# The feed-forward part of a hybrid decoder layer in two phases: gate and up for all feature pairs, then the down projection as seven block products

## Chip, cores and metric

One core of a Trainium2 chip runs the program. The metric is device microseconds per execution, lower is better; before and after are timed in several runs each, and the median counts.

## What is computed

One layer: a time-mixing part, a pooling part and an output projection give `h` (1024 tokens x 1024 features), and then this feed-forward part, on which the change works:

```python
D_FF = -(-8 * D_MODEL // (3 * 256)) * 256          # 2816 = 22 x 128
f = (jax.nn.silu(h @ ffn_gate[i]) * (h @ ffn_up[i])) @ ffn_down[i]
e = jax.nn.sigmoid(h @ pl_gate[i]) * (p[i] @ pl_proj[i])
h = layer_norm(ALPHA * h + f + e, ln2_g[i], ln2_b[i])
```

## The kernel before, in words

**Splits.** Every operand of a matmul is held as two `float32r` parts, high and low: `split` (line 789) casts the fp32 value on ScalarE (line 790) and subtracts the cast from it on VectorE (line 791). A product of two operands is then three matmuls (line 49): high x high, high x low, low x high. `wsplit` (799) splits into a tile of the pool `w`; `load` (794) brings 128x512 fp32 values into one of six `raw` buffers over SP's DMA queue. The numbers of buffers stand in `NB` (775): 6 `raw`, 4 `g`, 4 `pu`, 8 `w`, 4 `a`.

**Gate and up.** The 22 feature tiles of 128 go in 11 pairs. For each pair `gate_up` (961) calls `seven` (925) twice, for gate and for up. `seven` multiplies a 2x2 block matrix of weights (two feature tiles, two halves of the 1024 inputs) with a 2x2 block matrix of activations (input halves, token halves) by seven products where the plain way has eight: sums and differences of the weights are made on VectorE, those of the activations were made once (`tb1` to `tb4`), and each product is 12 matmuls of 128x512 into one PSUM bank. Gate uses the three banks of pool `mm`, up those of pool `dn` (five). VectorE adds the products into the four blocks of the result; gate goes through Silu on ScalarE, and up times gate is split at once (line 976) into the tiles `ahl`.

**Down.** `down` (995) takes a pair's two feature tiles: for each half `cf` of the 1024 outputs it loads and splits two weight tiles (`down_w`, 982), and for each of eight token tiles makes 6 matmuls into a bank (`down_tile`, 985), which VectorE adds into `acc` (line 993), the fp32 sum of 1024 tokens x 1024 outputs in SBUF. The down of a pair stands in `mid` (1029) of the next one, between its gate and its up; the last two pairs are done together at the end, 12 matmuls to a bank, with the final norm `fin` (1003) behind each token tile. `late` (1011) puts scale, bias and the embedding term onto `acc`, 16 VectorE instructions in each of three pairs.

**Order.** The engines run in program order each; the framework's scheduler sets that order when the program is built, and its semaphores make an instruction wait for what it reads and for buffers that come free. TensorE's list follows the code; the lists of VectorE, ScalarE and SP are interleaved.

Of the kernel before, what the change touches and what calls it, by code (L numbers as in the profile page):

```python
# [9 lines left out]
F32 = mybir.dt.float32  # L10
F32R = mybir.dt.float32r
AF = mybir.ActivationFunctionType
ALU = mybir.AluOpType
# [7 lines left out]
KT = 8  # L21
# [3 lines left out]
NFF = 22  # L25
# [17 lines left out]
def hybrid_layer(ctx, tc, x, pT, w_in, cols, rows, lora, gl, pool_w, w_out,  # L43
                 ff_gate, ff_up, ff_down, pl_proj, pl_gate, out, dbg=_no):
    nc = tc.nc
    V, S, G, PE = nc.vector, nc.scalar, nc.gpsimd, nc.tensor

    def mm(o, l, r, a, z):
        PE.matmul(o, lhsT=l, rhs=r, start=a, stop=z)  # L49
# [5 lines left out]
    dp = ctx.enter_context(tc.tile_pool(name="scr", bufs=2, space=DRAM))  # L55

    hp = ctx.enter_context(tc.tile_pool(name="act", bufs=4))
# [18 lines left out]
    for h in range(2):  # L76
        r = slice(64 * h, 64 * h + 64)
# [41 lines left out]
    e_d = dp.tile([T, D], F32, name="e_d", bufs=1)  # L119
    pe_d = dp.tile([T, D], F32, name="pe_d", bufs=1)  # L120
    m_d = dp.tile([T, D], F32, name="m_d", bufs=1)
    rkv_d = dp.tile([3 * NP, 128, 512], F32, name="rkv_d", bufs=1)
    st8 = cq.tile([128, NP, 64], F32, name="st8")
    mmp = ctx.enter_context(tc.tile_pool(name="mm", bufs=3, space=PSUM))

    def act_tiles(nm):
        return [hp.tile([128, KT, 512], F32R, name=f"{nm}{i}", tag="act") for i in range(4)]
# [631 lines left out]
    dnp = ctx.enter_context(tc.tile_pool(name="dnb", bufs=5, space=PSUM, reuse_waits="tile"))  # L759

    acc = [sp.tile([128, D], F32, name=f"acc{tt}", tag="acc", bufs=8) for tt in range(8)]
# [7 lines left out]
    for tt in range(4, 8):  # L769
        mix(tt)  # L770
    ostk.close()
    bp = ctx.enter_context(tc.tile_pool(name="bp", bufs=1, side="right", reuse_waits="tile"))


    NB = {"raw": 6, "g": 4, "pu": 4, "w": 8, "a": 4}
# [1 line left out]
    def small(tag, nm, dt=F32):  # L777
        return sp.tile([128, 512], dt, name=nm, tag=tag, bufs=NB[tag])

    def wide(tag, nm, dt=F32R):  # L780
        return sp.tile([128, 2, 512], dt, name=nm, tag=tag, bufs=NB[tag])

    def flat(t):
        return t.rearrange("p x c -> p (x c)")
# [4 lines left out]
    def split(h, l, r):  # L789
        S.copy(h, r)  # L790
        V.tensor_tensor(l, r, h.bitcast(F32), ALU.subtract)  # L791
        return h, l

    def load(src, nm):
        r = small("raw", nm)
        nc.sync.dma_start(r.rearrange("p (k c) -> p k c", c=src.shape[2]) if len(src.shape) == 3 else r, src)
        return r

    def wsplit(r, nm):
        t = wide("w", nm)  # L800
        return split(t[:, 0, :], t[:, 1, :], r)


    b12, b11, b21, b22 = act_tiles("h1")
# [7 lines left out]
    def brow(i, nm, tag):  # L812
        t = flat(wide(tag, nm, F32))
        nc.sync.dma_start(t, rows[i:i + 1, :].to_broadcast([128, D]))
        return t
# [21 lines left out]
    for i, k in enumerate((2, 3)):  # L837
        hl = [t23[:, 4 * i + 2 * x:4 * i + 2 * x + 2, :].rearrange("p c f -> p (c f)") for x in range(2)]
        for cf in range(2):
            r = load(w_out[128 * k:128 * k + 128, 512 * cf:512 * cf + 512], "w23r")  # L840
# [3 lines left out]
    for i in range(2):  # L844
        r = load(ya_d[2 + i, :, 512:1024], "y23")
        split(yh[:, 512 * i:512 * i + 512], yl[:, 512 * i:512 * i + 512], r)
    for tt in range(4, 8):
        for cf in range(2):
            cs = slice(512 * cf, 512 * cf + 512)
            ps = mmp.tile([128, 512], F32, name="pm", tag="mm")  # L850
            for i, (wh, wl) in enumerate(w23):
                tsl = slice(512 * i + 128 * tt - 512, 512 * i + 128 * tt - 384)
# [105 lines left out]
        evict(0, 1, prod(w3, b22, "p3"), u4, u4)  # L958
        evict(1, 0, prod(w4, tb4, "p4"), u3, u3)

    def gate_up(f, ahl, mid):
        g = {}

        def keep_gate(i, t, ps, u, c):
            d = g[i, t] = small("g", "gs")
            V.tensor_tensor(d, ps, u, ALU.add)  # L966
            S.activation(d, d, AF.Silu)

        def keep_up(i, t, ps, u, c):
            d = g[i, t]  # L970
            c = small("pu", "c") if c is None else c
            V.tensor_tensor(c, ps, u, ALU.add)
            V.tensor_tensor(d, c, d, ALU.mult)
            ah, al = ahl[i]
            sl = slice(512 * t, 512 * t + 512)
            split(ah[:, sl], al[:, sl], d)

        seven(ff_gate, f, lambda nm: mmp.tile([128, 512], F32, name=nm, tag="mm"), keep_gate)
        mid()
        seven(ff_up, f, lambda nm: dnp.tile([128, 512], F32, name=nm, tag="dn"), keep_up)  # L980

    def down_w(fs, cf):
        return [wsplit(load(ff_down[128 * f:128 * f + 128, 512 * cf:512 * cf + 512], "wdr"), "wd") for f in fs]

    def down_tile(ahl, ws, tt, cf):
        tsl = slice(128 * tt, 128 * tt + 128)
        cs = slice(512 * cf, 512 * cf + 512)
        ps = dnp.tile([128, 512], F32, name="pd", tag="dn")
        for n, ((ah, al), (wh, wl)) in enumerate(zip(ahl, ws)):
            mm(ps, ah[:, tsl], wh, n == 0, False)  # L990
            mm(ps, ah[:, tsl], wl, False, False)
            mm(ps, al[:, tsl], wh, False, n == len(ahl) - 1)
        V.tensor_tensor(acc[tt][:, cs], ps, acc[tt][:, cs], ALU.add)  # L993

    def down(fs, ahl):
        for cf in range(2):
            ws = down_w(fs, cf)
            for tt in range(8):
                down_tile(ahl, ws, tt, cf)

    grows = []

    def fin(tt):
        a = acc[tt]
        (m,), (rs,) = stats(sp, [a])
        V.scalar_tensor_tensor(a, a, m, grows[0], ALU.subtract, ALU.mult)
        V.scalar_tensor_tensor(a, a, rs, grows[1], ALU.mult, ALU.add)
        nc.sync.dma_start(out[128 * tt:128 * tt + 128, :], a)


    def late(f):
        if f not in (2, 4, 6):
            return
        for cf in range(2):
            cs = slice(512 * cf, 512 * cf + 512)
            r = None
            if f < 6:
                r = load(rows[1 + f // 2:2 + f // 2, cs].to_broadcast([128, 512]), "rw")
                S.activation(r, r, AF.Copy, scale=ALPHA)
            for tt in range(8):  # L1020
                a = acc[tt][:, cs]
                t = load(e_d[128 * tt:128 * tt + 128, cs], "er") if r is None else r
                V.tensor_tensor(a, a, t, ALU.mult if f == 2 else ALU.add)

    prev = []
    for f in range(0, NFF - 2, 2):
        ahl = [[None, None], [None, None]]

        def mid():
            late(f)  # L1030
            if prev:
                down(*prev.pop())
            for i in range(2):
                for x in range(2):
                    ahl[i][x] = flat(wide("a", "ahl"[0:2] + "hl"[x]))

        gate_up(f, ahl, mid)
        prev.append(((f, f + 1), ahl))


    f = NFF - 2
    ahl = [[None, None], [None, None]]

    def mid():
        t = hp.tile([128, KT, 512], F32R, name="alast", tag="act")
        for i in range(2):
            for x in range(2):
                ahl[i][x] = t[:, 4 * i + 2 * x:4 * i + 2 * x + 2, :].rearrange("p c f -> p (c f)")

    gate_up(f, ahl, mid)  # L1050
    (fs, ahl0), = prev
    ws = [down_w(fs, cf) for cf in range(2)]
    t = hp.tile([128, KT, 512], F32R, name="wlast", tag="act")
    for cf in range(2):
        for i in range(2):
            r = load(ff_down[128 * (f + i):128 * (f + i) + 128, 512 * cf:512 * cf + 512], "wdr")
            ws[cf].append(split(t[:, 4 * cf + 2 * i, :], t[:, 4 * cf + 2 * i + 1, :], r))
    grows += [brow(4, "g2", "w"), brow(5, "b2", "w")]
    for tt in range(8):
        for cf in range(2):  # L1060
            down_tile(ahl0 + ahl, ws[cf], tt, cf)
        fin(tt)


_SHAPES = [
# [46 lines left out]
```

## Time and profile before

| | us |
|---|---|
| median of 3 runs | 1390.58 (1387.95 to 1393.26) |
| the profiled execution | 1389.85 |
| its span in the trace | 1388.1 |
| TensorE matmul busy (PE) | 1333.3, 96% of the span |
| VectorE busy (DVE) | 1012.0, 73% |
| ScalarE busy (ACT) | 487.8, 35% |
| moved by DMA | 122.89 MB, 89 GB/s over the span |

PE is the matmul row of TensorE and PEld its weight loads, DVE is VectorE, ACT is ScalarE, SP the engine whose queue issues the DMAs. A busy share is an average over stages with different limits, so a stage is read by itself.

### The profile page before, as it was taken

Reading aid. Unit: us, or ns where it says so; the run is one execution under the profiler, and the core shown is the slowest. Engines: PE = TensorE matmul, PEld = TensorE weight load, DVE = VectorE, ACT = ScalarE, POOL = GpSimd, SP = SyncE. Lnnn points to the kernel's source line nnn. Section 1 sums busy time; section 2 is a strip of 40 time slices with the busy share of each in tenths; the row PEclk is TensorE's granted clock in tenths of the full one; section 3 lists DMA queues with packets and bytes.
Section 4 is the critical chain, followed back from the end, with each engine's and each line's share of the span. In section 5 each row is a group of like instructions: output and inputs, shape, how many; then the busy total and the mean of one; then the engine's idle time right before and its main releaser. Section 6 shows DMA issues by size and latency. Waiting matters only on the chain.

```text
span 1388.1 us, 22672 instructions
## 1 busy us (share of the span) xinstructions
PE 1333.3 (96%) x9160; PEld 1052.6 (76%) x9160; DVE 1012.0 (73%) x1769; ACT 487.8 (35%) x815; POOL 12.7 (1%) x48
## 2 busy tenths in 40 slices
PE   7999999998979989979999999999999999999997
PEld 5777777776657667858888888888888888888885
DVE  7936665589797953566999697876767667676688
ACT  6733433243435311277343231322323232232320
POOL 0000000000000000000000000000000000000000
PEclk9999999999999999999999999999999999999999
DMA  8522120312133251674332122411202111121212
GB/s 291 198 99 65 53 59 9 103 50 65 24 81 114 65 152 45 230 235 136 115 125 87 31 88 78 139 61 39 68 31 76 39 54 62 38 69 31 76 69 91
DMA packets 92473, 122.89 MB, mean 89 GB/s; under 512 B 31952, under 2 KB 41168, under 8 KB 92368
## 3 DMA queue, kind: packets, MB, share of 16 engines
q1 hardware_dynamic: 92224, 121.40, 27.6%
q8 instruction: 72, 1.18, 0.4%
q14 instruction: 33, 0.27, 0.1%
q10 hardware_dynamic: 144, 0.04, 0.0%
HBM read 91.53 MB, written 29.88 MB: 87 GB/s over the span
## 4 chain that ended last, share of the span: by engine, by line
PE 79%; DVE 10%; DMA 7%; ACT 3%; issue 1%; SPq 0%; DVEq 0%; ACTq 0%
PE p L49 31%; PE pd L49 17%; PE pz L49 9%; PE pgt L49 6%; PE pm L49 4%; PE py L49 2%; DMA o<-h_d 1%; PE cw L49 1%; PE pg L49 1%; PE cs L49 1%; DMA m_d<-o 1%; DMA cc<-d 1%; PE cu L49 1%; PE pe L49 1%; PE pzz L49 1%
## 5 line engine op out<-in xcount | busy, mean ns | idle before, releaser
L49 PE MATMUL p<-tb,p 128*128 128x512 f32 x1056 | 250.1, 392 | 0.0
L49 PEld LDWEIGHTS p<-tb,p 128*128 128x128 f32 x1056 | 198.5, 188 | 44.5
L49 PE MATMUL pd<-wd,ahh 128*128 128x512 f32 x640 | 197.7, 390 | 0.0
L49 PE MATMUL p<-h,p 128*128 128x512 f32 x792 | 191.3, 395 | 0.0
L49 PE MATMUL pz<-hT,wh 128*128 128x512 f32 x576 | 189.1, 403 | 0.0
L49 PEld LDWEIGHTS p<-h,p 128*128 128x128 f32 x792 | 149.1, 188 | 35.0
L993 DVE TENSOR_TENSOR acc<-pd,acc 128x512 f32<-128x512 f32 x160 | 110.2, 689 | 59.6 <-PE pd L49 59.2
L790 ACT CAST p<-a 128x512 fp32r<-128x512 f32 x132 | 81.6, 622 | 201.8 <-PE p L49 89.6
L49 PEld LDWEIGHTS pd<-wd,ahh 128*128 128x128 f32 x640 | 120.1, 188 | 25.5
L49 PEld LDWEIGHTS pz<-hT,wh 128*128 128x128 f32 x576 | 107.1, 188 | 31.7 <-issue 4.7
L49 PE MATMUL pd<-wd,ahl 128*128 128x512 f32 x320 | 124.7, 390 | 0.0
L49 PE MATMUL pz<-hT,wl 128*128 128x512 f32 x288 | 116.6, 405 | 0.0
L791 DVE TENSOR_TENSOR p<-a,p 128x512 fp32r<-128x512 f32 x132 | 90.5, 688 | 19.2 <-ACT p L790 19.1
L49 PE MATMUL pm<-wo,mh 128*128 128x512 f32 x224 | 77.4, 413 | 2.7 <-ACT wo L723 1.4
L49 PEld LDWEIGHTS pd<-wd,ahl 128*128 128x128 f32 x320 | 60.1, 188 | 12.7
L49 PEld LDWEIGHTS pz<-hT,wl 128*128 128x128 f32 x288 | 54.0, 188 | 15.5 <-issue 3.8
L947 DVE TENSOR_TENSOR u<-p,u 128x512 f32<-128x512 f32 x66 | 45.3, 687 | 17.5 <-PE p L49 17.5
L49 PE MATMUL pgt<-wg,h 128*128 128x512 f32 x192 | 50.0, 405 | 3.4 <-ACT wg L790 3.0
L49 PEld LDWEIGHTS pm<-wo,mh 128*128 128x128 f32 x224 | 41.4, 188 | 14.8 <-ACT wo L723 2.2
L234 DVE TENSOR_TENSOR wl<-wr,wh 128x512 fp32r<-128x512 f32 x36 | 24.7, 689 | 33.9 <-ACT wh L232 33.1
L966 DVE TENSOR_TENSOR gs<-p,u 128x512 f32<-128x512 f32 x44 | 30.4, 690 | 24.6 <-PE p L49 24.5
L790 ACT CAST p<-s 128x512 fp32r<-128x512 f32 x22 | 13.7, 621 | 97.6 <-PE pd L49 78.2
(285 smaller groups left out, 2073.9 us busy)
## 6 DMA issues: line engine op xcount, KB each, us to landing
a<-ff_gate SPq DMA_DIRECT2D x44, 256.0 KB, 2.7
a<-ff_up SPq DMA_DIRECT2D x44, 256.0 KB, 2.7
wdr<-ff_down SPq DMA_DIRECT2D x44, 256.0 KB, 2.7
wr<-w_in SPq DMA_DIRECT2D x36, 256.0 KB, 2.8
wgr<-pl_gate SPq DMA_DIRECT2D x24, 256.0 KB, 4.4
x<-x SPq DMA_DIRECT2D x8, 512.0 KB, 5.9
pe_d<-eo SPq DMA_DIRECT2D x16, 256.0 KB, 3.1
h_d<-x SPq DMA_DIRECT2D x8, 512.0 KB, 2.6
```

What stands on the lines that cost most here:

```text
L49: PE.matmul(o, lhsT=l, rhs=r, start=a, stop=z)
L234: V.tensor_tensor(wl, wr, wh.bitcast(F32), ALU.subtract)
L790: S.copy(h, r)
L791: V.tensor_tensor(l, r, h.bitcast(F32), ALU.subtract)
L947: V.tensor_tensor(t, ps, u, ALU.add)
L966: V.tensor_tensor(d, ps, u, ALU.add)
L993: V.tensor_tensor(acc[tt][:, cs], ps, acc[tt][:, cs], ALU.add)
```

## The change

`gate_up` runs for all 11 pairs with no down products between. The four 128x512 blocks of up times gate are not split but stored to DRAM, with three sums and differences of them that VectorE makes (`s12`, `s34`): seven parts `a_d[0..6]` per pair. In the second phase the down projection is itself a 2x2 block product (token halves, output halves, and the two feature tiles of a pair as the inner halves) by seven products. Each is summed in PSUM over all 11 pairs: 11 steps, in a step four token tiles of 128 (four banks, `px` or `py`) with three matmuls each. The products run in the order of the parts 0; 4 and 5 in turn, step by step; 6; 2; 1; 3, called first to seventh below. For a step the part is loaded again and split, the weights are loaded, for some products subtracted on VectorE, and split; the weight sums of the seventh (`t4`) are made during the second and third and kept in SBUF. Split operands go in turn into 30 places (`parts_of_two`). `into`, `all_into` and `up_to` add the finished products into `acc` or into the running sum `us`; the second product's result is copied to `p5` by ScalarE.

```diff
--- before.py
+++ after.py
@@ -119,6 +119,7 @@
     e_d = dp.tile([T, D], F32, name="e_d", bufs=1)
     pe_d = dp.tile([T, D], F32, name="pe_d", bufs=1)
     m_d = dp.tile([T, D], F32, name="m_d", bufs=1)
+    a_d = dp.tile([7, NFF // 2, 128, 512], F32, name="a_d", bufs=1)
     rkv_d = dp.tile([3 * NP, 128, 512], F32, name="rkv_d", bufs=1)
     st8 = cq.tile([128, NP, 64], F32, name="st8")
     mmp = ctx.enter_context(tc.tile_pool(name="mm", bufs=3, space=PSUM))
@@ -769,7 +770,8 @@
     for tt in range(4, 8):
         mix(tt)
     ostk.close()
-    bp = ctx.enter_context(tc.tile_pool(name="bp", bufs=1, side="right", reuse_waits="tile"))
+    bstk = ExitStack()
+    bp = bstk.enter_context(tc.tile_pool(name="bp", bufs=1, side="right", reuse_waits="tile"))
 
 
     NB = {"raw": 6, "g": 4, "pu": 4, "w": 8, "a": 4}
@@ -958,45 +960,40 @@
         evict(0, 1, prod(w3, b22, "p3"), u4, u4)
         evict(1, 0, prod(w4, tb4, "p4"), u3, u3)
 
-    def gate_up(f, ahl, mid):
+    def gate_up(n, mid):
+
+        f = 2 * n
         g = {}
 
         def keep_gate(i, t, ps, u, c):
             d = g[i, t] = small("g", "gs")
             V.tensor_tensor(d, ps, u, ALU.add)
             S.activation(d, d, AF.Silu)
+
+        def save(i, t):
+            nc.sync.dma_start(a_d[i, n], t)
 
         def keep_up(i, t, ps, u, c):
             d = g[i, t]
             c = small("pu", "c") if c is None else c
             V.tensor_tensor(c, ps, u, ALU.add)
             V.tensor_tensor(d, c, d, ALU.mult)
-            ah, al = ahl[i]
-            sl = slice(512 * t, 512 * t + 512)
-            split(ah[:, sl], al[:, sl], d)
+            if (i, t) != (0, 1):
+                save({(0, 0): 0, (1, 0): 1, (1, 1): 3}[i, t], d)
 
         seven(ff_gate, f, lambda nm: mmp.tile([128, 512], F32, name=nm, tag="mm"), keep_gate)
         mid()
         seven(ff_up, f, lambda nm: dnp.tile([128, 512], F32, name=nm, tag="dn"), keep_up)
-
-    def down_w(fs, cf):
-        return [wsplit(load(ff_down[128 * f:128 * f + 128, 512 * cf:512 * cf + 512], "wdr"), "wd") for f in fs]
-
-    def down_tile(ahl, ws, tt, cf):
-        tsl = slice(128 * tt, 128 * tt + 128)
-        cs = slice(512 * cf, 512 * cf + 512)
-        ps = dnp.tile([128, 512], F32, name="pd", tag="dn")
-        for n, ((ah, al), (wh, wl)) in enumerate(zip(ahl, ws)):
-            mm(ps, ah[:, tsl], wh, n == 0, False)
-            mm(ps, ah[:, tsl], wl, False, False)
-            mm(ps, al[:, tsl], wh, False, n == len(ahl) - 1)
-        V.tensor_tensor(acc[tt][:, cs], ps, acc[tt][:, cs], ALU.add)
-
-    def down(fs, ahl):
-        for cf in range(2):
-            ws = down_w(fs, cf)
-            for tt in range(8):
-                down_tile(ahl, ws, tt, cf)
+        s12, s34 = [wide("a", nm, F32) for nm in ("s12", "s34")]
+        a11, a12, a21, a22 = g[0, 0], g[1, 0], g[0, 1], g[1, 1]
+        V.tensor_tensor(s12[:, 0, :], a21, a22, ALU.add)
+        V.tensor_tensor(s12[:, 1, :], s12[:, 0, :], a11, ALU.subtract)
+        V.tensor_tensor(s34[:, 0, :], a11, a21, ALU.subtract)
+        save(4, s12[:, 0, :])
+        save(5, s12[:, 1, :])
+        save(2, s34[:, 0, :])
+        V.tensor_tensor(s34[:, 1, :], a12, s12[:, 1, :], ALU.subtract)
+        save(6, s34[:, 1, :])
 
     grows = []
 
@@ -1022,44 +1019,109 @@
                 t = load(e_d[128 * tt:128 * tt + 128, cs], "er") if r is None else r
                 V.tensor_tensor(a, a, t, ALU.mult if f == 2 else ALU.add)
 
-    prev = []
-    for f in range(0, NFF - 2, 2):
...
-        gate_up(f, ahl, mid)
-        prev.append(((f, f + 1), ahl))
...
+    for n in range(NFF // 2):
+        gate_up(n, lambda: late(2 * n))
+
+
+    NK = NFF // 2
+    bstk.close()
+    bq = ctx.enter_context(tc.tile_pool(name="bq", bufs=1, side="right", reuse_waits="tile"))
+    px = [mmp.tile([128, 512], F32, name="px", tag="mm") for i in range(3)]
+    px.append(dnp.tile([128, 512], F32, name="px", tag="dn"))
+    py = [dnp.tile([128, 512], F32, name="py", tag="dn") for i in range(4)]
+    t4 = bq.tile([128, NK, 512], F32, name="t4", tag="t4", bufs=1)
+
+    def parts_of_two():
+        while True:
+            for _ in range(8):
+                yield wide("w", "dw")
+            for _ in range(4):
+                t = hp.tile([128, KT, 512], F32R, name="da", tag="act")
+                for i in range(4):
+                    yield t[:, 2 * i:2 * i + 2, :]
+            for _ in range(6):
+                yield bq.tile([128, 2, 512], F32R, name="db", tag="db", bufs=6)
+
+    room = parts_of_two()
+
+    def two(r):
+        t = next(room)
+        return split(t[:, 0, :], t[:, 1, :], r)
+
+    def a_two(i, k):
+        return two(load(a_d[i, k], "ar"))
+
+    def w_raw(j, c, k):
+        f = 2 * k + j
+        return load(ff_down[128 * f:128 * f + 128, 512 * c:512 * c + 512], "wdr")
+
+    def step(ps, a, w, first, last, only=range(4)):
+        for i in only:
+            tsl = slice(128 * i, 128 * i + 128)
+            mm(ps[i], a[0][:, tsl], w[0], first, False)
+            mm(ps[i], a[0][:, tsl], w[1], False, False)
+            mm(ps[i], a[1][:, tsl], w[0], False, last)
+
+    def into(hf, cf, i, t):
+        d = acc[4 * hf + i][:, 512 * cf:512 * cf + 512]
+        V.tensor_tensor(d, t, d, ALU.add)
+
+    def all_into(hf, cf, ps):
+        for i in range(4):
+            into(hf, cf, i, ps[i])
+
+    us, p5 = [], []
+
+    def up_to(ps):
+        for i in range(4):
+            V.tensor_tensor(us[i], ps[i], us[i], ALU.add)
+
+    for k in range(NK):
+        step(px, a_two(0, k), two(w_raw(0, 0, k)), k == 0, k == NK - 1)
+    for i in range(4):
+        us.append(small("pu", "ud"))
+        S.copy(us[i], px[i])
+    for k in range(NK):
+        b1, b2 = [wide("a", "b12", F32) for _ in range(2)]
+        for j, b in enumerate((b1, b2)):
+            f = 2 * k + j
+            nc.sync.dma_start(flat(b), ff_down[128 * f:128 * f + 128, :])
+        V.tensor_tensor(b1[:, 0, :], b1[:, 1, :], b1[:, 0, :], ALU.subtract)
+        step(py, a_two(4, k), two(b1[:, 0, :]), k == 0, k == NK - 1)
+        V.tensor_tensor(b1[:, 1, :], b2[:, 1, :], b1[:, 0, :], ALU.subtract)
+        step(px, a_two(5, k), two(b1[:, 1, :]), k == 0, k == NK - 1)
+        V.tensor_tensor(t4[:, k, :], b2[:, 0, :], b1[:, 1, :], ALU.subtract)
+        if k == 1:
+            all_into(0, 0, us)
+    for i in range(4):
+        p5.append(small("g", "p5"))
+        S.copy(p5[i], py[i])
+    up_to(px)
+    for k in range(NK):
+        step(py, a_two(6, k), two(w_raw(1, 1, k)), k == 0, k == NK - 1)
+    all_into(0, 1, us)
+    all_into(0, 1, p5)
+    all_into(0, 1, py)
+    for k in range(NK):
+        r, r2 = w_raw(1, 1, k), w_raw(0, 1, k)
+        V.tensor_tensor(r, r, r2, ALU.subtract)
+        step(px, a_two(2, k), two(r), k == 0, k == NK - 1)
+    up_to(px)
+    all_into(1, 1, p5)
+    for k in range(NK):
+        step(py, a_two(1, k), two(w_raw(1, 0, k)), k == 0, k == NK - 1)
+    all_into(0, 0, py)
+    ops = [(a_two(3, k), two(t4[:, k, :])) for k in range(NK)]
+    all_into(1, 1, us)
+    all_into(1, 0, us)
+    grows += [brow(4, "g2", "a"), brow(5, "b2", "a")]
+    for i in range(4):
+        fin(i)
+    for i in range(4):
+        for k, (a, w) in enumerate(ops):
+            step(px, a, w, k == 0, k == NK - 1, (i,))
+        into(1, 0, i, px[i])
+        fin(4 + i)
 
 
 _SHAPES = [
```

Three places show how the lists of the engines move. The first is TensorE after the gate products of the second pair (`p` are products of gate and up, `pd` of down). Before:

```order
L49 MATMUL p_7552<-h_6165,p_7468 128x512 x12
L49 MATMUL p_7568<-tb_7117,p_7471 128x512 x12
L49 MATMUL pd<-wd,ahh 128x512 x2
L49 MATMUL pd<-wd,ahl 128x512
L49 MATMUL pd<-wd,ahh 128x512 x2
L49 MATMUL pd<-wd,ahl 128x512
```

With the change:

```order
L49 MATMUL p_7554<-h_6166,p_7470 128x512 x12
L49 MATMUL p_7570<-tb_7118,p_7473 128x512 x12
L49 MATMUL p_7643<-h_6164,p_7616 128x512 x12
L49 MATMUL p_7657<-h_6165,p_7619 128x512 x12
L49 MATMUL p_7674<-tb_6973,p_7626 128x512 x12
L49 MATMUL p_7689<-tb_6760,p_7633 128x512 x12
```

The up products of the pair now follow its gate products directly, where 96 down matmuls stood between. The second place is SP's list at the end of the last pair and the start of the second phase (`ar` is a part of `a_d` loaded again, `wdr` and `b12` are weights, `gs` and `s` are the last blocks and sums to be stored); with the change alone, since nothing answers to it before:

```order
L798 DMA ar_10707<-a_d_139 128x512
L974 DMA a_d_139<-s12_10514 128x512
L974 DMA a_d_139<-gs_10366 128x512
L974 DMA a_d_139<-s12_10514 128x512
L974 DMA a_d_139<-s34_10515 128x512 x2
L798 DMA wdr_10712<-ff_down 128x512
L798 DMA ar_10728<-a_d_139 128x512
L798 DMA wdr_10732<-ff_down 128x512
L798 DMA ar_10748<-a_d_139 128x512
L798 DMA wdr_10753<-ff_down 128x512
L1088 DMA b12_10777<-ff_down 128x1024
L1088 DMA b12_10778<-ff_down 128x1024
```

The last five stores of the first phase now stand among the loads of the first product, and the double-width weight loads of the second and third follow. The third place is ScalarE between the third and the fourth product (`da`, `db`, `dw` are places for split operands, `py` the banks that the second product leaves and the fourth needs), again with the change alone:

```order
L792 CAST db_11484<-ar_11482 128x512
L792 CAST db_11489<-wdr_11487 128x512
L792 CAST db_11506<-ar_11504 128x512
L792 CAST db_11511<-wdr_11509 128x512
L792 CAST db_11545<-ar_11543 128x512
L792 CAST db_11548<-wdr_11538 128x512
L1098 COPY p5_11284<-py_10532 128x512
L1098 COPY p5_11286<-py_10533 128x512
L792 CAST dw_11570<-ar_11568 128x512
L1098 COPY p5_11288<-py_10534 128x512
```

The copies out of `py` stand behind the casts of the fourth product's last two steps (`db_11484` to `db_11511`) and of the fifth's first (`db_11545`, `db_11548`), and so behind all 22 casts of the fourth product.

## Rows read from the trace of the kernel before

**Rows 1.** Chain that ended last, in order of time: start us, us, what.

```profile
650.98 59.92 PE pgt L49 x258
710.90 58.23 PE p L49 x252
769.13 21.78 PE pd L49 x96
790.91 38.84 PE p L49 x168
...
1254.09 21.78 PE pd L49 x96
1275.87 58.24 PE p L49 x252
1334.11 44.49 PE pd L49 x192
1379.32 1.19 DVE acc L1007
```

**Rows 2.** Busy time by stretch of the feed-forward part; columns in the first row.

```profile
core 0: us, PE busy (x) PEld busy (x) DVE busy (x) ACT busy (x) POOL busy (x), PEclk, DMA share, GB/s
...
710.90:769.13 58.23, 58.23 (x254) 47.42 (x253) 54.25 (x88) 26.58 (x44) 0.00 (x0) 1.00 0.31 100
769.13:790.91 21.78, 21.78 (x97) 18.02 (x97) 13.94 (x21) 3.10 (x5) 0.00 (x0) 1.00 0.10 33
790.91:829.75 38.84, 38.84 (x170) 31.60 (x169) 36.21 (x59) 15.21 (x26) 0.00 (x0) 1.00 0.25 75
...
1275.87:1334.11 58.24, 58.24 (x254) 47.40 (x253) 40.88 (x64) 21.33 (x37) 0.00 (x0) 1.00 0.22 73
1334.11:1378.60 44.49, 44.48 (x193) 35.59 (x191) 41.37 (x75) 3.97 (x9) 0.00 (x0) 1.00 0.17 71
```

**Rows 3.** Groups by line: busy us, mean ns of one, idle before and its releasers.

```profile
L993 DVE TENSOR_TENSOR acc<-pd,acc 128x512 f32<-128x512 f32 x160 | 110.2, 689 | 59.6 <-PE pd L49 59.2
L790 ACT CAST wd<-wdr 128x512 fp32r<-128x512 f32 x40 | 24.8, 622 | 30.7 <-PE p L49 15.5 <-issue 11.8 <-DMA wdr<-ff_down 3.4
L137 DVE BATCH_NORM_STATS2 st<-acc 128x6 f32<-128x512 f32 x32 | 21.3, 685 | 1.6 <-DMA acc<-m_d 1.2
L951 ACT COPY u<-p 128x512 f32<-128x512 f32 x22 | 12.9, 587 | 29.4 <-PE p L49 29.4
L1006 DVE SCALAR_TENSOR_TENSOR acc<-acc,mv,g 128x1024 f32<-128x1024 f32 x8 | 10.3, 1284 | 0.3
```

**Rows 4.** Timeline of VectorE where nothing makes it wait: start us, us, instruction.

```profile
669.57 0.68 DVE L895 TENSOR_TENSOR t<-t,h 128x512 f32<-128x512 f32 x1
670.17 0.69 DVE L898 TENSOR_TENSOR t<-h,h 128x512 f32<-128x512 f32 x1
670.77 0.68 DVE L896 TENSOR_TENSOR t<-t,h 128x512 f32<-128x512 f32 x1
```

**Rows 5.** Busy time by stretch where transfers are dense, columns as in rows 2.

```profile
10.00:20.00 10.00, 9.53 (x38) 6.58 (x38) 8.62 (x18) 5.68 (x11) 0.00 (x0) 1.00 0.85 288
...
30.00:40.00 10.00, 7.71 (x41) 5.85 (x40) 7.38 (x14) 9.17 (x15) 0.00 (x0) 1.00 0.98 315
585.00:595.00 10.00, 6.62 (x35) 5.44 (x34) 2.84 (x5) 2.67 (x4) 0.00 (x0) 0.96 0.63 211
595.00:605.00 10.00, 4.62 (x24) 3.17 (x23) 5.54 (x9) 9.49 (x16) 0.00 (x0) 0.84 0.63 187
605.00:615.00 10.00, 9.77 (x34) 7.38 (x35) 7.60 (x12) 6.75 (x12) 0.00 (x0) 0.86 0.84 277
615.00:625.00 10.00, 10.00 (x45) 8.14 (x45) 7.76 (x14) 6.56 (x11) 0.00 (x0) 1.00 0.77 245
```

**Rows 6.** The casts of line 790 alone in one stretch: us, ACT busy, clock, DMA share, GB/s.

```profile
603.40:625.30 21.90, 13.32 (x22) 0.92 0.77 250
```

**Rows 7.** Timeline of ScalarE there: idle before, and its releaser, in brackets.

```profile
606.93 0.62 ACT L790 CAST wgh<-wgr 128x512 fp32r<-128x512 f32 x1 [1.36 <-DMA wgr<-pl_gate]
```

**Rows 8.** DMA issues: size of one, median us from issue to landing.

```profile
wdr<-ff_down SPq DMA_DIRECT2D x44, 256.0 KB, 2.7
...
wgr<-pl_gate SPq DMA_DIRECT2D x24, 256.0 KB, 4.4
```

More of the change, by code (lines that the diff above doesn't have):

```diff
@@ L1023, in late @@
                 V.tensor_tensor(a, a, t, ALU.mult if f == 2 else ALU.add)
-    prev = []
-    for f in range(0, NFF - 2, 2):
[L1027 to L1035, printed above, removed]
-        gate_up(f, ahl, mid)
-        prev.append(((f, f + 1), ahl))
-    f = NFF - 2
-    ahl = [[None, None], [None, None]]
@@ L1044, in mid @@
[L1044 to L1062, printed above, removed]
+    for n in range(NFF // 2):
[5 more added lines that the diff above has]
+    px.append(dnp.tile([128, 512], F32, name="px", tag="dn"))
```

## Prediction

> **What bounds the kernel now.** I read the chain of waits in order of time first. From 710.90 to 1378.60 us, the whole feed-forward part, it is one engine, TensorE: runs of gate and up products (`p`) alternate with runs of down products (`pd`), nothing between them [rows 1]. The table by stretch says the same: PE is busy for 58.23 of 58.23 us, 21.78 of 21.78, 38.84 of 38.84, at a granted clock of 1.00, which is the 2.4 GHz level [rows 2]. So a matmul less is worth its full pace there, and nothing else is worth anything until it makes TensorE wait. The pace from these rows: 168 `p` in 38.84 us are 231.2 ns each; 96 `pd` in 21.78 us are 226.9; the last 192 `pd` in 44.49 us are 231.7. (The mean of 390 ns in a list by line is one matmul's latency; they overlap.) Behind the last matmul lie 1388.1 - 1378.6 = 9.5 us of VectorE and output.
>
> The sum is made against the profiled execution, 1389.85 us, 1.75 us of it outside the span; it lies 0.7 us below the median of the runs shown, inside their spread.
>
> **What it removes.** All down products of before: nine runs of 96 and one of 192 [rows 1], 1056 matmuls in 9 x 21.78 + 44.49 = 240.5 us. With them go 160 additions into `acc` [rows 3].
>
> **What it adds.** Seven products, each 11 steps (one per pair) x 4 token tiles x 3 matmuls = 132, so 924. Same 128x512 form, so bounds are the two paces, 226.9 and 231.7: 209.7 to 214.1 us. The pattern (same weight-side pair, two moving tiles) lies between both rows, so I take 229.5: 212.1 us. The balance is -28.4 us (-30.8 to -26.4). Gate and up keep their 1848 matmuls and the tail is unchanged. Without any new wait the time would be 1389.85 - 28.4 = 1361.5.
>
> **Phase 1: gate and up without the down run between.** The down run gave VectorE rest (13.94 of 21.78 us busy). Now a pair has 18 + 22 VectorE instructions in its two sevens and 4 sums where 4 splits were: 44 per 38.84 us, with `late` 16 more in three pairs, 60. Back to back VectorE starts one every 0.60 us, though each lasts 0.69 [rows 4]: 44 are 26.4 us, 60 are 36.0, both below 38.84. And before has this very sequence twice: three sevens on end from 710.90, with 88 VectorE instructions in 58.23 us, and again from 1275.87, with TensorE busy throughout [rows 2]. 60 in 38.84 is 1.54 per us, the 59 and 88 shown are 1.52 and 1.51. I cost phase 1 at nothing. Cover gone: if the 60 went at 0.69 us each, three pairs would lose 41.4 - 38.84 each, 7.7 us in all; that is the upper bound. Below nothing is excluded, as TensorE has no gap there to win. The seven stores per pair and eight loads are 3.9 MB in 38.84 us, 101 GB/s, small beside the transfer rates below.
>
> **Phase 2: VectorE and ScalarE.** The 11 steps of a product need both operands split, one ScalarE cast (622 ns) and one VectorE subtraction each, and some a difference first. In the whole phase VectorE has 237 instructions of 128x512, 142 us at 0.60 and 163 at 0.69, and eight final norms of two statistics and two long passes, 8 x (2 x 0.69 + 2 x 1.28) = 32 us [rows 3]: 174 to 195 against 212 us of TensorE. That is cover on the mean. There are 30 places for split operands, 15 steps of lead (8 `w`, 16 `act`, 6 `db`), so the stages with much VectorE work (second and third product, 7 per two steps) live on lead gained in the first.
>
> **Phase 2: the one place where a wait can stand.** The fourth product needs the four PSUM tiles `py` that the second leaves, and ScalarE copies them out. The copies stand on ScalarE's queue behind the casts of the whole fourth product and of the fifth's first step (the order at that place, in the part on the change). So by the time TensorE has run three products, 396 x 0.2295 = 90.9 us, all these operands must have been loaded. In loads of 0.262 MB (128x512 f32): first product 22; second and third 22 for activations and 44 for weights (two loads of 128x1024 per step); fourth 22; fifth's first step 3; 113 in all. By SP's order 16 of them stand ahead of the first product's start, and five stores among the rest: 102 x 0.262 = 26.7 MB in 90.9 us, 294 GB/s asked for.
>
> What rate can it get? Early in the kernel, with SP's queue full, 288 and 315 GB/s at busy shares of 0.85 and 0.98 [rows 5]. The nearest row in kind is 603.4 to 625.3: there the same six `raw` buffers feed the same cast and subtraction, 22 casts in 21.9 us at 250 GB/s [rows 6], and ScalarE waits on the loads [rows 7], which take 4.4 us to land there against 2.7 in the quiet feed-forward part [rows 8]. In phase 2 four 512 KB buffers are in flight beside the six, so I take a row of a full queue, 288: 26.7 / 0.288 = 92.7 us, 1.8 late, then two casts and the copy, 0.62 + 0.62 + 0.59 = 1.8 [rows 3]. That is 3.6 us of wait. The bounds: at 315 it takes 84.8 us and nothing is late; at 250, 107 us, 16 late and 18 of wait. VectorE must do 123 instructions by then: 74 to 85 us, in time. After the fourth product's start its operands lie ready for 30 us, so lead comes back and I expect no further wait: the last product's operands need 22 places, and places and VectorE are free during the sixth.
>
> The Trainium skill's DMA: Bandwidth & Descriptors (Specifications) gives a core about 358 GB/s from HBM. By that figure the 26.7 MB would take an estimated 75 us and no wait would stand; the trace reached 315 at a share of 0.98, and no run here shows more, so the sum stays with the rows.
>
> **The sum**: 1389.85 - 28.4 + 3.6 = 1365 us.
>
> **Rivals.**
> *No wait at all* (loads at 315 GB/s or the lead is longer): 1361 us. For it: four 512 KB buffers in flight; the share had room in the early rows. Chance 0.22. The Trainium skill's 358 GB/s, quoted above, would give this case.
> *VectorE binds*: phase 1 loses 7.7 us in the pairs with `late`, since casts and evictions do not leave it back to back: 1365 + 7.7 = 1373. Against it stands the sequence already shown without a gap. Chance 0.13.
> *The loads of phase 2 bind* (the one that can end slower): the ring of six buffers holds the rate at what such work showed [rows 6]. At 250 GB/s the wait is 18 us, and TensorE comes back slower: between 595 and 615 its clock was granted at 0.84 and 0.86 on the mean after it had been busy only 4.62 of 10 us, and the second stretch holds 34 matmuls where 45 fit, 11 x 0.23 = 2.5 us [rows 5]. So 1361.5 + 18 + 2.5 = 1382. At 211, 127 us of loading: 36 late, 40 us with the rest, 1402. It decides for slower than before when the wait passes 28.4 us, below some 232 GB/s; below 219 it is slower by over 0.5%. Chance 0.20, of that 0.08 below 219. For it: landing times rise with load [rows 8]. Against: that stretch also waits for a `wgh` buffer and a table load.
> *The change does not remove what it says*: excluded; TensorE's list holds 84 matmuls per seven as before, then 924.
>
> **How the numbers follow.** Forecast 0.45, no wait 0.22, VectorE 0.13, loads 0.20. 0.5% of the median, 7 us, is about what a measurement of this kernel can tell from no change. The first three cases are all faster by more, and 0.06 of the fourth: 0.86. Between 219 and some 248 GB/s lies no change: 0.06. Slower: 0.08. The range reaches from 1358, below the no-wait case at the faster pace (1359), to 1386, which takes in the loads at 250 GB/s and leaves out some 0.12 above and a little below.
>
> **What would show it.** Right: 924 matmuls `px` and `py` in 210 to 216 us of TensorE time; gate and up unbroken for 427 us; one gap of a few us before the fourth product's first `py`, ended by ScalarE's copy `p5`, with ScalarE waiting on loads of the fourth product ahead of it; DMA at 280 to 315 GB/s from the first to the third product. Wrong: gaps of TensorE inside phase 1 ended by VectorE; gaps at many steps of the second and third product ended by casts that wait for loads; a pace of `px` outside 226 to 232 ns.

## The result and the profile after

The changed kernel takes 1359.97 us (median of 4 runs, 1357.09 to 1362.55), the kernel before, run beside it, 1391.61 (4 runs): a ratio of 0.9771, 95% interval 0.9756 to 0.9787. That is faster, 5 us under the 1365 forecast and inside the range. The profiled execution was the longest of the four, 1362.55 us with a span of 1360.8.

The chain of waits of the changed kernel, in order of time, as [rows 1] has it for before:

```profile
714.69 415.89 PE p L49 x1800
...
1130.65 0.63 ACT dw L792
...
1231.69 0.69 DVE wdr L1107
1232.38 0.61 DVE acc L1067
1233.00 0.57 ACT p L1098
1233.57 0.04 issue
1233.61 28.90 PE py L49 x126
1262.51 29.94 PE px L49 x132
```

The alternation of `p` and `pd` is gone: one block of `p`, then the products `px` and `py` of 132 matmuls. The chain leaves TensorE once, from 1130.58 to 1233.57 us. There it goes through loads, VectorE and ScalarE, while TensorE does the end of `p` and the first three products; where the chain comes back to it, before 1233.61, TensorE waits. Busy time by stretch (columns in the first row) answers to [rows 2]:

```profile
core 0: us, PE busy (x) PEld busy (x) DVE busy (x) ACT busy (x) POOL busy (x), PEclk, DMA share, GB/s
714.69:1141.48 426.79, 426.79 (x1849) 347.55 (x1848) 340.25 (x536) 143.12 (x236) 0.00 (x0) 1.00 0.36 120
1141.48:1171.50 30.02, 30.02 (x134) 24.84 (x133) 25.59 (x42) 14.37 (x25) 0.00 (x0) 1.00 0.91 320
1171.50:1201.50 30.00, 30.00 (x134) 24.83 (x133) 28.73 (x47) 14.05 (x26) 0.00 (x0) 1.00 0.93 320
1201.50:1231.30 29.80, 29.80 (x133) 24.67 (x132) 24.18 (x38) 19.77 (x34) 0.00 (x0) 1.00 0.87 293
1231.30:1262.30 31.00, 30.24 (x133) 24.69 (x132) 25.14 (x41) 10.22 (x19) 0.00 (x0) 1.00 0.76 244
1262.30:1352.45 90.15, 90.15 (x397) 74.18 (x396) 73.69 (x130) 31.47 (x56) 0.00 (x0) 1.00 0.41 138
```

PE is busy without a break in phase 1 and, but for 0.8 us in the fifth row, in phase 2. All waits of TensorE from 714 to 1353 us are one:

```profile
PE py L49 <- ACT p L1098: 0.8, 1, 0.8
```

(columns: us in total, times, longest; from start to start of the matmuls it is 1.0 us more than their pace). The balance against the profiled execution of before: the feed-forward part begins 3.8 us later (714.69 against 710.90 in [rows 1]; nothing before it was changed, and over the runs of this study it began between 709 and 717 us), its TensorE part takes 637.8 us instead of 667.7, and the tail 8.4 instead of 9.5. 3.8 - 29.9 - 1.1 = -27.2; the spans differ by 27.3.

### The profile page after: what moved, and what is told of

It reads as the page before. It is cut to its first block, busy times and chain, and to the rows that moved or that the text cites. A ratio compares the mean times of both kernels' runs of the same rounds, so it can differ in the third digit from the quotient of the medians.

```text
span 1360.8 us, 22957 instructions
## 1 busy us (share of the span) xinstructions
PE 1310.2 (96%) x9028; PEld 1033.7 (76%) x9028; DVE 1025.9 (75%) x1807; ACT 528.6 (39%) x889; POOL 12.7 (1%) x48
## 4 chain that ended last, share of the span: by engine, by line
PE 72%; DVE 13%; DMA 10%; ACT 2%; issue 2%; SPq 0%; DVEq 0%; ACTq 0%
PE p L49 31%; PE pz L49 10%; PE py L49 6%; PE pgt L49 6%; PE px L49 4%; PE pm L49 3%; DMA wdr<-ff_down 2%; PE pg L49 2%; DMA o<-h_d 1%; PE cw L49 1%; PE pzz L49 1%; DMA ar<-a_d 1%; PE pe L49 1%; PE cs L49 1%; DMA m_d<-o 1%
## 5 line engine op out<-in xcount | busy, mean ns | idle before, releaser
L49 PE MATMUL px<-da 128*128 128x512 f32 x276 | 64.2, 389 | 0.0
L49 PEld LDWEIGHTS px<-da 128*128 128x128 f32 x276 | 51.8, 188 | 10.8
L49 PE MATMUL py<-da 128*128 128x512 f32 x204 | 47.6, 389 | 0.0
L49 PEld LDWEIGHTS pgt<-wg,h 128*128 128x128 f32 x192 | 37.4, 197 | 12.1 <-ACT wg L792 3.0
L49 PE MATMUL pm<-wo,ml 128*128 128x512 f32 x112 | 46.0, 413 | 0.0
L49 PEld LDWEIGHTS py<-da 128*128 128x128 f32 x204 | 38.3, 188 | 8.0
```

## Experiments

The theory: the gain is the 132 matmuls that the down part no longer does, at TensorE's pace, since nothing else became late. Its open points were what phase 1 and phase 2 hide and how near they are to their limits. Each run was set against the kernel before; what is said of the changed kernel is from its trace above.

**Is it the matmuls, or the split into phases?** `e1_plain_down` keeps both phases and makes the down part by the plain product: four stores per pair, no sums, four blocks in turn.

```diff
-            if (i, t) != (0, 1):
-                save({(0, 0): 0, (1, 0): 1, (1, 1): 3}[i, t], d)
+            save(2 * t + i, d)
...
-        s12, s34 = [wide("a", nm, F32) for nm in ("s12", "s34")]
...
+    def plain(ps, hf, cf, fs, last):
+        for f in fs:
+            a = two(load(a_d[2 * hf + f % 2, f // 2], "ar"))
+            w = two(w_raw(f % 2, cf, f // 2))
+            step(ps, a, w, f == 0, last and f == 2 * NK - 1)
```

> Two phases kept, but the down part as the plain block product: four parts of the activations stored as they are, no sums, 4 blocks of 22 steps x 12 = 1056 matmuls instead of 924. If the gain of the change comes from its 132 matmuls alone: 132 x 0.227 = 30 us above the changed kernel, less its 1 us wait, so 1389 us, within 0.5% of the kernel before (ratio 0.996 to 1.001). If the split into two phases brings a gain of its own (a better pace, fewer small waits): below 1380, ratio under 0.992. If DRAM traffic or the second phase costs something that the seven products hide: above 1396.

1390.39 us (10 runs), ratio 0.9984 (0.9971 to 0.9998): the whole gain is given back. Its stretches (columns as above), phase 1 and phase 2:

```profile
709.41:1136.20 426.79, 426.79 (x1849) 347.54 (x1848) 320.12 (x497) 142.84 (x236) 0.00 (x0) 1.00 0.31 101
1136.20:1376.04 239.84, 239.84 (x1057) 198.06 (x1055) 145.06 (x240) 97.56 (x172) 0.00 (x0) 1.00 0.60 193
```

Phase 1 is the same, 426.79 us, with 497 VectorE instructions as with 536, so the sums and stores for the seven products cost nothing there. Phase 2 is 239.8 us, 227 ns for each of 1056, against 240.5 for the `pd` of before. Splitting into phases is worth about 1 us (the two rows together are 666.6 us, the feed-forward part of before 667.7); the 132 matmuls are worth 239.8 - 211.0 = 28.8.

**How far is phase 1 from VectorE's limit?** `e2_vector76` adds 32 VectorE operations to each pair without `late`.

```diff
+    def more(n, t):
+        if n not in (1, 2, 3):
+            for _ in range(4):
+                V.tensor_tensor(t, t, t, ALU.max)
```

> 32 more 128x512 VectorE operations (t = max(t, t), values unchanged) in each of the eight pairs without late: 76 per pair of 38.84 us. If VectorE starts one every 0.60 us: 45.6 us per pair, 6.8 over, 8 x 6.8 = 54 us longer, about 1415. If one costs its listed 0.69 us: 52.4, 13.6 over, 109 us longer, about 1469. If VectorE has more room than that (76 still fit under TensorE): no more than 2 us longer, 1362. It says how far phase 1 stands from being bound by VectorE.

1428.82 us. Phase 1 in one row, and the waits of TensorE in it:

```profile
710.00:1197.50 487.50, 443.35 (x1853) 356.10 (x1852) 473.58 (x777) 136.49 (x237) 0.00 (x0) 0.95 0.31 102
```

```profile
PE p L49 <- ACT p L792: 31.3, 5, 7.5
PE p L49 <- DVE p L793: 12.7, 2, 10.6
```

VectorE is busy for 473.58 us with 777 instructions, 0.61 us each, not the 0.69 of a single one. Phase 1 is 60 us longer where 0.60 gave 54. With 76 in a pair the splits (lines 792, 793) come late; with 60 in 38.84 us, as the pairs with `late` have in the changed kernel, TensorE does not wait. So the step from 60 to 76 per pair holds the limit, where 38.84 / 0.61 = 64 would put it.

**Does the transfer rate set the wait before the fourth product?** `e3_more_load` adds 33 loads that nobody reads over the first three products.

```diff
+    def extra(k):
+        nc.sync.dma_start(small("g", "ex"), ff_down[128 * k:128 * k + 128, 0:512])
```

> 33 more loads of 128x512 f32 (8.65 MB) that nobody reads, over the first three products of phase 2: 35.4 MB instead of 26.7 before the fourth product's copies. If the transfer rate sets the wait there: at 311 GB/s (seen in the changed kernel at 0.90 busy) 114 us of loading against 90 of matmuls, some 24 us of waits in the second to fourth product, 1384; if the queue reaches 345 (311 / 0.90), 103 us, 13 us of waits, 1373. If ScalarE's order or the places for operands set it and not the rate: at most 2 us, 1360 to 1362.

1366.27 us in one run. Of its 6 us over the median of the changed kernel 0.2 stand in phase 2, which takes 211.2 us as against 211.0; its `p` began at 716.6 us, and its tail is 10 us. The second 30 us of phase 2, then the first three products together in this run and in the changed kernel:

```profile
1173.40:1203.40 30.00, 29.89 (x132) 24.39 (x131) 25.20 (x41) 12.76 (x23) 0.00 (x0) 1.00 1.03 389
```

```profile
1143.40:1233.60 90.20, 90.09 (x397) 74.21 (x396) 66.41 (x106) 37.05 (x67) 0.00 (x0) 1.00 0.97 354
```

```profile
1141.50:1231.30 89.80, 89.80 (x397) 74.32 (x396) 78.48 (x125) 48.18 (x84) 0.00 (x0) 1.00 0.90 311
```

389 GB/s where the changed kernel had 320: the transfers had room, and something else held the rate of the changed kernel. But the run does not show that the wait is free of the rate. The loads that are read came later than in the changed kernel: 87 us into phase 2 SyncE's timeline has 95 of them issued, there 116, and ScalarE has done 67 instructions where it did 84. That TensorE waits no longer has another reason. The scheduler moved ScalarE's `p5` copies too: they stand behind 67 casts of the phase, in the changed kernel behind 90 and 91, and here they wait for `py` and not for loads:

```profile
1229.77 2.06 ACT L1103 COPY p<-py 128x512 f32<-128x512 f32 x4 [2.58 <-PE py L49]
```

The wait on `p5` is gone, and 0.5 us on VectorE's `dw` stand in its place. What the extra loads would have cost at the order of the changed kernel stays open.

**Does the ring of six buffers hold the rate?** `e4_six_buffers` takes the wide buffers away: the same bytes in 256 KB loads through `raw`.

```diff
-        b1, b2 = [wide("a", "b12", F32) for _ in range(2)]
...
-            nc.sync.dma_start(flat(b), ff_down[128 * f:128 * f + 128, :])
+        (x1, y1), (x2, y2) = [[w_raw(j, c, k) for c in range(2)] for j in range(2)]
```

> The weights of the second and third product come as four loads of 128x512 through the six raw buffers, instead of two of 128x1024 through four buffers beside them: the same bytes with six loads in flight. My rival (the ring of six holds the rate at the 250 GB/s that such work showed early in the kernel): 107 us for 26.7 MB, 16 to 18 us of waits, 1378 to 1381. If the loads are not held by the ring (311 GB/s as with the larger buffers): no more than 2 us longer, 1360 to 1363.

1373.30 us, and phase 2 takes 222.7 us, 11.7 more. Three of its stretches with 3.4 us behind a wait, and the waits of TensorE:

```profile
1140.40:1170.40 30.00, 30.00 (x134) 24.83 (x133) 21.15 (x33) 11.18 (x19) 0.00 (x0) 1.00 0.86 283
1170.40:1205.40 35.00, 34.70 (x153) 28.18 (x152) 24.80 (x39) 12.67 (x23) 0.00 (x0) 1.00 0.68 223
1205.40:1241.00 35.60, 28.87 (x115) 21.95 (x113) 23.24 (x37) 14.91 (x27) 0.00 (x0) 0.95 0.72 236
...
1242.19:1245.60 3.41, 3.41 (x9) 2.65 (x9) 3.41 (x7) 3.08 (x7) 0.00 (x0) 0.50 0.69 234
```

```profile
PE py L49 <- ACT p L1095: 3.9, 1, 3.9
PE py L49 <- ACT db L792: 1.5, 1, 1.5
PE py L49 <- ACT dw L792: 0.7, 1, 0.7
...
PE px L49 <- ACT ud L1083: 0.3, 1, 0.3
```

The rival lives: at 223 and 236 GB/s with the DMA engines at 0.68 and 0.72, the loads are late. The listed waits, two of 0.3 us on VectorE among them, sum to 7.0 us. Of the other 4.7 about 3.2 are 16 matmuls behind two of the waits that start 0.427 us apart: the granted clock is 0.50 there, the 1.2 GHz level. The rest is smaller delays behind the waits. ScalarE's order moved here as well, the `p5` copies stand behind 75 to 77 casts, but the longest wait is on them all the same. What saves the changed kernel is the four 512 KB buffers beside the six; whether by their number or by the larger loads was not separated.

**Would more buffers end the wait?** `e7_ten_buffers` gives the activations of the first three products the four `g` buffers; `e8_ten_later` has `(4, 5)` in the place of `(0, 4, 5)`, the second and third alone.

```diff
     def a_two(i, k):
+        if i in (0, 4, 5):
+            r = small("g", "ag")
+            nc.sync.dma_start(r, a_d[i, k])
+            return two(r)
         return two(load(a_d[i, k], "ar"))
```

> The activations of the first three products are loaded through four buffers of their own (the g ones, free until p5) and no longer through the six raw ones: ten small buffers instead of six. If the number of buffers in flight sets the rate of phase 2 (as the runs with six and with extra loads say): above 340 GB/s from the first product on, operands ready well before the fourth product, its wait of 1 us gone, 924 matmuls in 210 us, 1359. If the buffers are enough as they are: 311 to 320 GB/s and the wait of about 1 us as before.

1368.24 us: a new hole, 8.2 us, at the start of phase 2, and none before the fourth product.

```profile
PE px L49 <- ACT dw L792: 7.8, 1, 7.8
```

SyncE's queue there (start us, us, instruction) shows why: the first `ag` loads go out at 1140.81, behind all stores of the last pair, because a `g` buffer comes free only when that pair's up is done; phase 1 had ended at 1137.3.

```profile
1133.83 0.33 SPq L974 DMA_DIRECT2D a_d<-gs  x1
...
1136.88 1.52 SPq L974 DMA_DIRECT2D a_d<-s  x2
1139.41 0.32 SPq L974 DMA_DIRECT2D a_d<-gs  x1
1139.77 0.93 SPq L974 DMA_DIRECT2D a_d<-s  x2
1140.81 2.01 SPq L1054 DMA_DIRECT2D ag<-a_d  x4
```

> As the run with ten buffers, but only the second and third product take their activations through the four g buffers; the loads of the first product stay in the six raw ones, so SyncE's queue no longer stands behind a g buffer that the last pair of phase 1 gives back late. If that order made the 8 us hole at the start of phase 2 and the number of buffers made the wait before the fourth product: no hole, no wait, TensorE without a gap over 0.3 us from the first p to the last px, 924 matmuls in 210 us, 1359. If the hole came from ten loads in flight as such: it is there again, 1366 or more. If the wait before the fourth product is ScalarE's order alone: 1 us, as in the changed kernel.

1362.99 us: the hole is gone, so it was that order. But the wait stays (1.7 us listed, twice ScalarE's `p5` copies), at 326, 307 and 294 GB/s over the first three products. Four more small buffers do not speed the loads up. In the changed kernel SyncE waits here, from 1141 to 1190 us, most of all for VectorE to finish with a 512 KB buffer (line 1088, the `b12` loads), and VectorE is busy for 28.73 of 30.00 us in the stretch from 1171.50:

```profile
SPq L1088 <- DVE t L1093: 15.0, 7, 4.2
SPq L798 <- DVE da L793: 3.7, 6, 1.1
```

Whether VectorE's time or the number of wide buffers is the last cause of that 1 us was not separated: over the first three products the chain of the changed kernel goes 44 us through loads and 35 us through VectorE, in turns. In e7, with ten buffers, TensorE comes to the fourth product some 11 us later, 8 of the hole and 3 of matmuls behind it at a granted clock of 0.50, and no wait is left. Nor was ScalarE's order tried by itself, and it is the nearest rival. In the changed kernel ScalarE stands idle for 1.14 us ahead of the cast that holds up the last two copies (its timeline is shown below); copies start 0.48 us apart, so both would have fitted in there by my estimate, and TensorE would not have waited.

**What sets the pace of a matmul?** Gate and up ran at 231.0 ns on the mean, `px` and `py` at 226.9, the same form on the same clock. Two layouts were tried first.

```diff
-                mm(ps, w[0][:, ks], b[:, 4 + k, :], False, False)
+                mm(ps, w[0][:, ks], b[:, 2 * k + 1, :], False, False)
```

> The high and low halves of the token operands of the gate and up products stand side by side (2 KB apart, as those of the down operands do) instead of 8 KB apart. The gate and up products ran at 231.1 ns a matmul in the changed kernel, the down products at 226.9. If the distance of the halves makes the difference: 226.9 for all 1848, 4.2 x 1848 = 7.8 us less, 1352. If the order of the sums (12 matmuls in a row into one PSUM tile with new moving data each) or something else does: 231, no change, 1358 to 1363.

1363.12 us (4 runs), ratio 0.9796 (0.9769 to 0.9823); `p` still at 231.0. The distance of the halves is not it.

```diff
-    b12, b11, b21, b22 = act_tiles("h1")
+    b12, b22, b21, b11 = act_tiles("h1")
```

> Two of the four tiles of token operands change places in SBUF (b11 and b22). In the changed kernel p1 (b11), p2 (b21) and p4 ran at 229 to 230 ns a matmul and p6, p7, p5 and p3 (b22) at 231.6 to 232.7. If the place of the moving tile decides: p1 goes to 232 and p3 to 229, the time stays. If the place in the order of the seven products decides: p1 stays at 229, p3 at 232. No change of the time in either case, 1358 to 1363.

1362.01 us, 231.0 again. The split that the expectation tells of the changed kernel had been read with a wrong starting matmul; read rightly it is in all three kernels the same: p6, p7 and p5, whose moving tiles are in the pool `bp`, at 229 to 230, p1, p2, p3 and p4, whose tiles are in `hp`, at 232 to 233. So the two tiles that changed places lay in one pool, and this run could not tell. The next runs move the pools themselves.

```diff
+    V.memset(cp.tile([128, 8], F32, name="pad8", tag="pad8", bufs=1), 0.0)
     hp = ctx.enter_context(tc.tile_pool(name="act", bufs=4))
```

> 32 bytes more ahead of the token operands' pool in SBUF: its tiles begin at byte 2112 (a multiple of 64) instead of 2080. In the two runs on places the products with moving tiles of that pool (b11, b21, b22, tb4) ran at 231.7 to 232.9 ns a matmul, those of the other pool (tb1 to tb3) at 229, whichever tile lay where within the pool. If the alignment of the tiles makes that: 229 for all seven, 1056 x 3.5 = 3.7 us less, 1357. If not: 231.0 on the mean, 1358 to 1363.

> 64 bytes ahead of the pool instead of 32 (its tiles begin at byte 2144). With 32 bytes the 1848 gate and up matmuls went from 231.0 to 233.3 ns, those on tb1 to tb3 too, whose own place did not move, so the place of the weight tiles counts. If the offset within 64 bytes decides, it is that of the changed kernel again: 231.0, 427 us of gate and up, 1358 to 1363. If a larger unit decides: another pace, between 226.9 (419 us, 1352) and 233.3 (431 us, 1366).

> 96 bytes ahead of the pool (its tiles begin at byte 2176, a multiple of 128). If the offset within 64 bytes decides, it is that of the run with 32 bytes: 233.3 ns, 431 us of gate and up, 1363 to 1368. If the offset within 128 bytes decides: another pace than both, between 226.9 (419 us, 1352) and 233.3.

1366.81, 1361.54 and 1364.99 us, `p` at 233.3, 230.6 and 233.3 ns, for 32, 64 and 96 bytes (`[128, 8]`, `[128, 16]`, `[128, 24]`). The timeline of TensorE in one of the last sevens, rows of consecutive matmuls of one kind (start us, us, instruction): in the changed kernel

```profile
1102.67 5.73 PE L49 MATMUL p<-h,p 128*128 128x512 f32 x24
1108.24 8.41 PE L49 MATMUL p<-tb,p 128*128 128x512 f32 x36
1116.49 2.96 PE L49 MATMUL p<-h,p 128*128 128x512 f32 x12
```

with 64 bytes of padding

```profile
1101.58 5.76 PE L49 MATMUL p<-h,p 128*128 128x512 f32 x24
1107.18 8.34 PE L49 MATMUL p<-tb,p 128*128 128x512 f32 x36
1115.36 2.95 PE L49 MATMUL p<-h,p 128*128 128x512 f32 x12
```

From start to start, 36 matmuls on `tb2`, `tb3`, `tb1` take 8.25 us (229.2 ns) in the first and 8.18 (227.2, and 226.7 within p7 and p5) in the second; 24 on `b11`, `b21` take 5.57 and 5.60. The bytes at which the tiles begin, read from the built programs and taken modulo 512, put this in order:

| padding | weights (`w`) | `tb` | ns | `b11`, `b21` | ns |
|---|---|---|---|---|---|
| none | 416 | 480 | 229.2 | 32 | 232.1 |
| 32 | 448 | 480 | 233.3 | 64 | 233.3 |
| 64 | 480 | 480 | 227.2 | 96 | 233.3 |
| 96 | 0 | 480 | 233.3 | 128 | 233.3 |

Fast is the one place where the two operands begin at the same offset. It fits phase 2, where both operands of a step come from one kind of place: 226.7 to 227.8 ns on the mean in every run, waits left out. So the last run makes all offsets equal:

```diff
+    V.memset(cp.tile([128, 112], F32, name="pad8", tag="pad8", bufs=1), 0.0)
     hp = ctx.enter_context(tc.tile_pool(name="act", bufs=4))
...
     sp = ctx.enter_context(tc.tile_pool(name="b", bufs=2, reuse_waits="tile"))
+    V.memset(sp.tile([128, 32], F32, name="pad9", tag="pad9", bufs=1), 0.0)
```

> 448 bytes ahead of the token operands' pool and 128 more ahead of the weight tiles' pool, so that all operand tiles of the gate, up, gating and down matmuls begin at the same byte modulo 512 (480). In the padded runs the products on tb1 to tb3 ran at 226.7 ns where weight tile and moving tile agreed modulo 512 (64 bytes of padding), 229.0 where they lay 64 apart, 233.3 at 32; the down products, whose two operands come from one kind of tile, always at 226.7 but for the matmuls where the kind changes (229 to 236). If the agreement sets the pace: all 1848 gate and up matmuls at 226.7 to 226.9, 7.7 us less there, some 2 us less in the 384 gating matmuls (232.3 ns now), about 1350, ratio to the kernel before 0.969 to 0.972. If it was the distance from the other pool alone: the products on b11, b21, b22 and tb4 stay at 232 to 233 and it is 1356 to 1361.

1351.01 us (5 runs, 1349.00 to 1352.99), ratio 0.9713 (0.9694 to 0.9731), below the interval of the changed kernel. The same place of its timeline, and its two phases:

```profile
1111.22 5.60 PE L49 MATMUL p<-h,p 128*128 128x512 f32 x24
1116.66 8.32 PE L49 MATMUL p<-tb,p 128*128 128x512 f32 x36
1124.82 2.88 PE L49 MATMUL p<-h,p 128*128 128x512 f32 x12
```

```profile
710.64:1130.26 419.62, 419.44 (x1849) 346.80 (x1848) 339.61 (x539) 141.55 (x238) 0.00 (x0) 1.00 0.36 122
1130.26:1341.54 211.28, 210.20 (x925) 173.10 (x923) 176.97 (x295) 90.01 (x158) 0.00 (x0) 1.00 0.67 227
```

24 matmuls in 5.44 us and 36 in 8.16: 226.7 ns on both kinds. 1848 in 419.6 us instead of 426.8 is 7.2 us; the gating products before (`pgt`) went from 232.3 to 226.7, 384 of them, 2 us. With the changed program this is the version to keep.

## Why the prediction was right, point by point

- **TensorE bounds the feed-forward part; a matmul less is worth its pace.** Right, and shown from both sides: e1 puts the 132 matmuls back and the gain is gone (0.9984).
- **Removed, 240.5 us; added, 924 at 229.5 ns, 212.1 us.** The pace was mis-sized: 226.9, the lower bound, so 924 took 209.7 and with the wait 211.0. I took the pace from "the pattern between both rows", which was no reason: both operands of `px` begin at the same offset, and the pad runs have the faster pace just there. 2.4 us of the error.
- **Phase 1 at nothing.** Right: 426.8 us, no gap, against 427 forecast. That VectorE starts one every 0.60 us [rows 4] held under load (0.61 in e2), so the bound of 7.7 us was the wrong one of the two.
- **One wait before the fourth product, on ScalarE's `p5` copies behind casts that wait for loads.** The place and the kind of chain were right. The timeline of the changed kernel there (start us, us, instruction, idle before it):

```profile
1229.20 0.62 ACT L792 CAST db<-ar 128x512 fp32r<-128x512 f32 x1 [1.59 <-DMA ar<-a_d]
1229.72 0.62 ACT L792 CAST db<-wdr 128x512 fp32r<-128x512 f32 x1
1230.24 1.06 ACT L1098 COPY p<-py 128x512 f32<-128x512 f32 x2
...
1232.45 0.62 ACT L792 CAST dw<-ar 128x512 fp32r<-128x512 f32 x1 [1.14 <-DMA ar<-a_d]
...
1232.98 1.06 ACT L1098 COPY p<-py 128x512 f32<-128x512 f32 x2
1233.61 1.66 PE L49 MATMUL py<-dw 128*128 128x512 f32 x6 [0.76 <-ACT p L1098]
```

  Two copies stand behind the fifth product's first step (the two casts at 1229.20 and 1229.72) and are in time. The other two stand behind the first cast of its second step, which waits 1.14 us for its load, and TensorE waits for them. (The chain shown with the result names VectorE's addition at 1232.38 ahead of the copy. By ScalarE's list it is the cast: the copy starts 0.53 us behind it, as one does behind the other there.) The size was wrong, 3.6 us forecast and 1.0 measured, and the steps that failed are in the count. The sum put all four copies behind the 113 loads up to the first step, and charged two casts and a copy from the start of the product on. The copies that made the wait needed load 116, though (`dw_11570` stands between them in the order on record), and one cast; and TensorE needs the third bank only six matmuls into the product. Load 116 had landed 91.0 us after phase 2 began: 105 transfers, 27.5 MB at 302 GB/s on the mean, where the sum had 26.7 MB at 288 and 92.7 us. That 288 came so near is luck. I took it as the rate of a full queue, but the transfers can do 389 (e3); the buffers beside the six hold the rate up (e4).
- **Tail unchanged, 9.5 us.** 8.4 in this execution, 10 in e3: it moves by 1.6 between executions.
- **The sum.** 1365 stood against 1362.55 for the profiled execution: -2.4 pace, -2.6 wait, -1.1 tail, +3.8 from a later start of the part that nothing changed. So the 2.5 us between them are in part luck: the two mis-sized terms make 5.0, which is also what 1365 is above the median.
- **Rivals.** No wait at all (1361) came nearest to the time; the wait was 1.0 us. VectorE binding (1373) did not happen, but e2 shows it 16 operations per pair away at most. Loads binding (1382) did not happen because of the wide buffers: e4, without them, has the 250 GB/s of [rows 6] nearly (223 to 236), waits of 7.0 us and, as that rival had it, matmuls at the lower clock behind them, about 3.2 us where I put 2.5. The Trainium skill's DMA: Bandwidth & Descriptors (Specifications) gives a core about 358 GB/s; e3's 389 over 30 us is more. The Trainium skill's HBM Reference (Specifications (TRN2)) says that a core alone goes well above that share, and the trace agrees.

## What to carry to other kernels

Where one engine is busy without a gap, fewer instructions on it are worth their pace, and the work is to show that what feeds it keeps up: count VectorE by its start-to-start time, and loads by the buffers that they wait for, since bytes over a rate hold only where the buffers let the queue run at that rate. An edit can also move the order of another engine's list, as e3 did with the copies: look at that list before a run's time is read as an answer. A load that needs a late buffer holds up every load behind it on its queue (e7). And compare the pace of the same matmul in different places of a trace: a difference of 2% was a matter of where the tiles begin.

## Unexpected of the hardware

The pace of a 128x512 `float32r` matmul depends on the byte offsets in SBUF of its two operands: 226.7 ns where both began at the same byte modulo 512, 229 at 64 bytes apart, 232 to 233.3 at 32 or 128 apart. e9 to e12 show this for offsets from 0 to 480; why it is so, and whether 512 is the unit (128 is too small, as the column of `b11` shows), the runs do not tell. Nor is it the whole rule: the last run of down products in the kernel before, whose matmuls go back and forth between two kinds of places, had 231.7 ns, and its order was not tried by itself.
